# Query copies tied behind the preceding softmax, merge loads tied to other weights, gated sums on GpSimd

## The chip, the cores and the metric

The kernel runs on one core of one Trainium2 chip. The metric is the time of one execution on the device in microseconds; the time before is the median of 3 runs, 2679.12 us (2677.36 to 2681.72).

## The reference

One encoder layer for 2048 tokens of width 1024, all in float32:

```python
h = rms_norm(x, norm_mix)
z = h @ w_in                     # 1024 -> q_a 512, k_a, v_a 128 each, q_b, k_b, v_b 512 each, gates 2 x 1024
y_a = windowed_gqa(q_a, k_a, v_a, sink)      # 8 heads, 2 key heads, |t-s| <= 128, ALiBi, a sink logit
y_b = neighborhood_attn(q_b, k_b, v_b, rpb)  # 8 heads on a 32 x 64 grid, 8 x 16 neighbours, position bias
merged = sigmoid(g_a + b) * (y_a @ w_proj_a) + sigmoid(g_b + b) * (y_b @ w_proj_b)
x = x + merged @ w_out
h2 = rms_norm(x, norm_mlp)
x = x + square(relu(h2 @ w_up)) @ w_down     # 1024 -> 4096 -> 1024
return rms_norm(x, norm_final)
```

## The kernel before

Every float32 product is made of three matmuls of rounded parts (`mm3`, L201: high by high, high by low, low by high). ScalarE rounds a tile to its high part, VectorE (in places GpSimd) subtracts it from the tile for the low part (`split`, L276; the attention's `ph` and `pl`). The four large projections (in, gate, up and down in part, out) use seven block products in place of eight, with sums of blocks made ahead by VectorE; the out-projection's seven are run in the order n = 1, 2, 5, 6, 3, 7, 4.

The stages follow one another on TensorE: in-projection (to 525 us), attention A (32 units of 4 heads by 128 queries), attention B (32 units of a head by a group of columns, with four row groups as its four tiles), merge (gating and out-projection, once per half m of the tokens), up, down. In attention A and B, matmuls of the gates and of the first out-going projection are put in between as fill work (tiles `mm`, `z`).

A scheduler places the instructions. It runs the program on a model of the engines and issues what is ready; the result is a fixed order for each engine, and on the chip each engine takes its instructions strictly in that order. `tc.issue_after(ins)` tells the scheduler to place what follows behind `ins` in the order of the engine that `ins` is on, with no semaphore. Tiles come from rings: a load into a ring's buffer waits until the buffer's last reader is through. Loads are issued by SyncE, in order, and each waits for the one before it on the same of eight semaphores, taken in turn.

An attention unit loads its queries (`load_q`, `q`, a ring of 3 buffers). The tile has two copies, z = 0 as loaded and z = 1 with the upper and the lower 64 partitions swapped and the halves apart; `turn_q` makes z = 1 with one copy on ScalarE (L834) and one on VectorE (L835). For each of four tiles a matmul with z = 0 and one with z = 1 make scores in a bank `s` (a ring of 3 banks); VectorE adds the bias and takes the maximum (L863 in A, L1112 in B), ScalarE negates it (L866, L1115) and takes the exponential with its sum (L870, L1118), VectorE makes the reciprocal (L872, L1120), and GpSimd scales the four tiles (L874, L1123). Then TensorE transposes the tile in pieces (`pt`), ScalarE and VectorE split those (`ph` L900, `pl` L901; in B `phb` L1159, `plb` L1160), and TensorE multiplies them with V (`av`). In B, GpSimd also makes the bias tables (L1078).

In the merge, `gated(f)` makes 128 features for 1024 tokens: loads of the gate `zg` and of the other branch's gated product `zp` (tiles `z`, 4 and 2 buffers), 24 matmuls with a slice of `w_pb`, the gate times the product on VectorE (L1640), and the sum of both into `m` (L272). `out_operands` makes the operands of the out-projection from `m` (`pgl`, weights `wo_d`), `out_products` multiplies, and VectorE adds the result to the rows of x (`xr`, L272). Finished rows are stored (`x2d`), normalised (L230 to L241), and turned by VectorE's transposes in groups g of 256 features into `h2d` (`turned_out`, L253). `beside_out(m)` is stepped once for each n; in m = 1 it steps `up_right`, which prepares up's left weights (`uraw`, `ubh`).

Of the kernel before, what the change touches and what calls it, by code (L numbers as in the profile page):

```python
# [8 lines left out]
F32 = mybir.dt.float32  # L9
# [13 lines left out]
P = 128  # L23
KC = D // P
NB = 4
BT = 512
# [66 lines left out]
def encoder_layer(ctx, tc, x, norm_mix, w_in, b_gate, sink, rpb, w_pa, w_pb, w_out,  # L93
# [733 lines left out]
    def load_q(pl, tag, src):  # L827

        q = T(pl, [P, 2, 4, P], F32R, tag, 3)
        return q, SY.dma_start(q[:, 0].bitcast(F32), src).ins  # L830

    def turn_q(q):

        A.copy(q[0:64, 1], q[64:128, 0].bitcast(F32))  # L834
        V.tensor_copy(out=q[64:128, 1], in_=q[0:64, 0].bitcast(F32))  # L835

    kas = [T(ap_, [P, S], F32R, f"ka{g}", 1) for g in range(2)]
    vas = [T(ap_, [P, 16, P], F32R, f"va{g}", 1) for g in range(2)]
# [5 lines left out]
    def attn_a(u, g, i):  # L844
        c0, c1 = (1 if i == 0 else 0), (2 if i == 15 else 3)
        lo, hi = c0 * P, c1 * P
        n = hi - lo
        if bias_a[g] is None:
            make_bias_a(g)
        base = (i - 1) * P  # L850
        q, ins = load_q(ap_, "qa", qs_a[g][i // 8][:, :, i % 8])
        began.append(ins)
        yield
        turn_q(q)
        ka, v = kas[g], vas[g]
        s = T(ap_, [P, 4, 384], F32, "sa", 4)
        st = T(ap_, [P, 8, 4], F32, "sta", 8)
        mx, nm, sm, es, ri = (st[:, k, :] for k in range(5))
        for h in range(4):
            ps = psum("s", 3)  # L860
            for z in range(2):
                PE.matmul(ps[:, :n], q[:, z, h, :], ka[:, base + lo : base + hi], start=z == 0, stop=z == 1)
            V.tensor_tensor_reduce(out=s[:, h, lo:hi], in0=ps[:, :n], in1=bias_a[g][:, h, lo:hi], scale=1.0,  # L863
                                   scalar=sink_t[:, 4 * g + h : 4 * g + h + 1], op0=ALU.add, op1=ALU.max,
                                   accum_out=mx[:, h : h + 1])
        A.activation(nm, mx, AF.Copy, scale=-1.0)  # L866
        V.tensor_tensor(out=es, in0=sink_t[:, 4 * g : 4 * g + 4], in1=mx, op=ALU.subtract)
        A.activation(es, es, AF.Exp)
        for h in range(4):
            A.activation(s[:, h, lo:hi], s[:, h, lo:hi], AF.Exp, bias=nm[:, h : h + 1], accum_out=sm[:, h : h + 1])  # L870
        V.tensor_tensor(out=sm, in0=sm, in1=es, op=ALU.add)
        V.reciprocal(ri, sm)  # L872
        for h in range(4):
            G.tensor_scalar(s[:, h, lo:hi], s[:, h, lo:hi], ri[:, h : h + 1], 0.5, ALU.mult, ALU.mult)  # L874
        yield
        po = [None]

        def result(c, ph, pl):
            if c == c0:
                po[0] = psum("av", 2)  # L880
            PE.matmul(po[0], v[:, i - 1 + c, :], ph, start=c == c0, stop=False)
            PE.matmul(po[0], v[:, i - 1 + c, :], pl, start=False, stop=c == c1 - 1)
            if c < c1 - 1:
                return
            e = u % 2 * 64
            t = (ya if u % 4 < 2 else yb)[e : e + 64]
            A.copy(t, po[0][64 - e : 128 - e, :])
            V.tensor_tensor(out=t, in0=po[0][e : e + 64, :], in1=t, op=ALU.add)
            flush(queue=SY)
            put(y_a[g].rearrange("(h d) t -> d h t", d=64)[:, :, i * P : (i + 1) * P],  # L890
                t.rearrange("d (h q) -> d h q", h=4))

        for c in range(c0, c1):
            pt = psum("pt", 2)
            for h in range(4):
                last = PE.transpose(pt[:, h * P : (h + 1) * P], s[:, h, c * P : (c + 1) * P], ident).ins
            marks.append(last)
            ph = T(ap_, [P, 512], F32R, "ph", 3)
            pl = T(ap_, [P, 512], F32R, "pl", 3)
            A.copy(ph, pt)  # L900
            V.tensor_tensor(out=pl, in0=pt, in1=ph.bitcast(F32), op=ALU.subtract)  # L901
            behind(lambda c=c, ph=ph, pl=pl: result(c, ph, pl))
# [143 lines left out]
    bp = pools(s_b, "right", ("masks", "braw0", "biass", "stb", "kb0", "qb", "biasl", "braw1", "kb1"), "b")  # L1046
    bp.update(pools(s_b, "left", ("sb0", "sb1", "vb0", "vb1", "sb2", "vb2", "phb", "plb"), "b"))
    boff, bstart, btotal = bias_layout()
    last_exp, n_raw = [None], [0]
    masks = T(bp, [P, btotal], F32, "masks", 1)  # L1050
    with tc.issue_after(began[20]):
        SY.dma_start(masks, mask_b)
# [36 lines left out]
    def attn_b(n_u, h, j, k, bias):  # L1089
# [25 lines left out]
        A.activation(nm, mx, AF.Copy, scale=-0.125)  # L1115
        for i in range(4):
            n = B_NR[i] * w
            last_exp[0] = A.activation(s[i][:, :n], s[i][:, :n], AF.Exp, bias=nm[:, i : i + 1], scale=0.125,  # L1118
                                       accum_out=sm[:, i : i + 1]).ins
        V.reciprocal(ri, sm)  # L1120
        for i in range(4):
            n = B_NR[i] * w
            G.tensor_scalar(s[i][:, :n], s[i][:, :n], ri[:, i : i + 1], 0.5, ALU.mult, ALU.mult)  # L1123
# [228 lines left out]
    def up_right(m):  # L1352
# [3 lines left out]
        def block(b, j, p):  # L1356
            SY.dma_start(b, h2d[2 * m + j][p * BT : (p + 1) * BT, :].rearrange("(k p) t -> p k t", p=P))
            if m:
                for k in range(4):
                    by_gain(b[:, k], 4 * p + k)  # L1360
            return b
# [13 lines left out]
        def gained(t, p):  # L1375
            for k in range(4):
                by_gain(t[:, k], 4 * p + k)
# [34 lines left out]
        yield  # L1412
        with tc.issue_after(last_left[0]):
            gained(t, 0)
            gained(b12, 0)
        b22 = block(up_rings["raw"](), 1, 1)
        gained_less(t, b22, 1, t)
        parts(6, t)
# [95 lines left out]
        yield  # L1514

    ORDER_O = (1, 2, 5, 6, 3, 7, 4)
    wo_dma, last_left = [None], [None]

    def out_operands(ms):

# [61 lines left out]
    def beside_out(m):  # L1582

        loads = load_y(1) if m == 0 else up_start()
        for n in range(7):
            if n == 1:
                with tc.issue_after(wo_dma[0]):
                    rows[1].extend(x_row(m, 1, t) for t in range(4))
            elif m == 0 and n in (3, 5):
                y_behind[0] = wo_dma[0]  # L1590
                state["y"] = next(loads)
            elif m == 1 and n:
                if n < 5:
                    next(loads)
                elif n == 6:
                    free = [T(p4x, [P, 2, 2, BT], F32, f"m{t}", 1).rearrange("p a b c -> p a (b c)") for t in (0, 1)]
                    turned_last(0, lambda g: free[g // 2][:, g % 2])
            yield

    def x_row(m, i, t):  # L1600
        row0 = (2 * m + i) * BT + t * P
        return load_tile(p4x, "xr", 8, xf[row0 : row0 + P])

    def turned_last(i, own):

        for g in range(4):
            turned_out(h2d[2 + i], own(g), rows[i], g)

    state = {"y": next_y}
# [1 line left out]
    for m in range(2):  # L1611
        ys = state["y"]
        ms = [T(p4x, [P, 2, 2, BT], F32, f"m{i}", 1) for i in range(4)]
        hls = {}
        operands = out_operands(ms)
        n_g = [0]
        old, rows = rows, [[], []]

        def gated(f):

            with tc.issue_after(wo_dma[0]) if m and f < 4 else nullcontext():
                gated_at(f)

        def gated_at(f):

            if f % 2 == 0:
                hls[f // 2] = slice_of([(cols(w_pb[0], (f + i) * P), 4) for i in range(2)])
            hl, c0 = hls[f // 2], 4 * (f % 2)
            g, ga = T(wp, [P, 2, BT], F32, "z", 4), T(p4, [P, 2, BT], F32, "z", 2)
            for j in range(2):  # L1630
                SY.dma_start(g[:, j], zg[2 * m + j][1][f * P : (f + 1) * P, :])
            for j in range(2):
                last_dma[0] = SY.dma_start(ga[:, j], zp[2 * m + j][f]).ins
            for j in range(2):
                ps = bank_at(n_g[0] % 4)
                n_g[0] += 1
                for c in range(4):
                    t = ys[j][c // 2]
                    mm3(ps, hl[:, 0, c0 + c, :], hl[:, 1, c0 + c, :], t[:, 0, c % 2], t[:, 1, c % 2], c == 0, c == 3)
                V.scalar_tensor_tensor(out=g[:, j], in0=g[:, j], scalar=1.0, in1=ps, op0=ALU.add, op1=ALU.mult)  # L1640
            add(V, ms[f // 2][:, f % 2], ga, g)

        for f in range(8):
            if m:
                i = f // 4
                turned_out(h2d[i], T(p4x, [P, 2 * BT], F32, "ht", 1), old[i], f % 4)
            gated(f)
            if f == 3:
                with tc.issue_after(last_dma[0]):
                    ready = [next(operands), next(operands)]  # L1650
            if f >= 4:
                with tc.issue_after(last_dma[0]):
                    rows[0].append(x_row(m, 0, f % 4))
        if m == 1:
            s_pg.close()
            s_w.close()

        def all_operands():
            yield from ready
            yield from operands  # L1660

        beside = beside_out(m)
        out_products(m, all_operands(), rows, beside)
# [8 lines left out]
        right = next(rights)  # L1672
    for _ in rest:
        pass
    turned_last(1, lambda t: hu())
    s_hu.close()
    s_wo.close()
    up_homes("bh3", "chunk", "bh7", "bh4")
    for m in range(2):
        if m:  # L1680
            right = next(rights)
# [203 lines left out]
```

## Time and profile before

| | |
|---|---|
| median of 3 runs | 2679.12 us (2677.36 to 2681.72) |
| profiled execution | 2687.74 us |
| its span in the profile | 2686.0 us |
| mean granted TensorE clock | 0.987 |
| busy: TensorE, VectorE, ScalarE, GpSimd | 2574.7, 1743.1, 1351.5, 355.8 us |
| in-projection, attention A, attention B | 0 to 525, 525 to 815, 815 to 1160 us |
| merge, up, down | 1160 to 1440, to 2068, to 2686 us |

The page gives each engine's busy time and the chain of work that ended last. A group's row reads: line, engine, operation, output and inputs with shapes, count, busy time, mean duration in ns, then the engine's idle time just before these instructions and what ended it. A row of the waits reads: engine, tile, line, what ended the wait, the total in us, how often, the longest. A row of the windows gives for each engine the busy time and the count of instructions, then the clock (1.00 is full), the busy share of the DMA engines and their rate. A timeline's row begins with start and duration in us.

### The profile page before, as it was taken

To read this page: it belongs to the slowest core of one execution; us is meant where nothing else is said; L and a number is where in the kernel's file an instruction comes from. 1 tells how busy PE (TensorE), PEld (TensorE's weight loads), DVE (VectorE), ACT (ScalarE), POOL (GpSimd) and SP (SyncE) were. 2 spreads that over 40 slices of the span, in tenths; PEclk is the share of its full clock that TensorE was granted. 3 is DMA by queue.
4 is the path that set the end of the run, shared out by engine and by line. 5 is a ranking of instruction groups with operands and counts; after the bars stand their busy time and mean duration, and the time that the engine had idled before them with its cause. 6 is when DMAs were issued, how large, how long until landed. Compare 5 with 4: busy or idle time off the path is not lost.

```text
span 2686.0 us, 34629 instructions
## 1 busy us (share of the span) xinstructions
PE 2574.7 (96%) x11936; PEld 2128.8 (79%) x11936; DVE 1743.1 (65%) x2781; ACT 1351.5 (50%) x2409; POOL 355.8 (13%) x482
## 2 busy tenths in 40 slices
PE   7999999989999989999999999999999999999998
PEld 5788888867777777788777788888887888888887
DVE  8856677566665666656577766786666535545766
ACT  6365555467766665532426555554445233322444
POOL 1001001133345645300000000000000000000001
PEclk9999999999999999999999999999999999999999
DMA  5767778753335676567996765764436935445555
GB/s 181 222 203 254 254 249 271 233 156 93 83 109 170 183 234 198 179 223 262 321 331 210 262 215 205 260 232 145 165 110 231 325 137 172 143 149 171 179 193 169
DMA packets 345776, 542.73 MB, mean 202 GB/s; under 512 B 31688, under 2 KB 151992, under 8 KB 344448
## 3 DMA queue, kind: packets, MB, share of 16 engines
q1 hardware_dynamic: 328416, 499.99, 57.4%
q10 hardware_dynamic: 10944, 24.12, 2.5%
q0 software_dynamic: 6240, 16.40, 1.9%
q8 instruction: 94, 1.54, 0.2%
q14 instruction: 82, 0.67, 0.1%
HBM read 353.69 MB, written 186.71 MB: 201 GB/s over the span
## 4 chain that ended last, share of the span: by engine, by line
PE 73%; DMA 11%; DVE 7%; ACT 4%; issue 3%; SPq 1%; POOL 0%; ACTq 0%; DVEq 0%; POOLq 0%
PE b L283 15%; PE b L282 15%; PE b L281 15%; PE zb L281 4%; PE zb L283 4%; PE zb L282 4%; DMA qb<-qs_b 4%; PE mm L202 2%; DMA qa<-qs_a 2%; PE mm L203 2%; PE mm L204 2%; PE av L1133 1%; PE b L202 1%; PE b L203 1%; PE b L204 1%
## 5 line engine op out<-in xcount | busy, mean ns | idle before, releaser
L282 PE MATMUL b<-dwh,dah 128*128 128x512 f32 x896 | 348.7, 389 | 0.4 <-DVE dwh L278 0.4
L283 PE MATMUL b<-dwh,dah 128*128 128x512 f32 x896 | 347.7, 389 | 0.0
L281 PE MATMUL b<-dwh,dah 128*128 128x512 f32 x896 | 338.4, 389 | 1.7 <-ACT dwh L277 1.7
L277 ACT CAST dah<-da 128x1024 fp32r<-128x1024 f32 (+1 forms) x128 | 121.1, 947 | 367.6 <-PE b L283 245.0
L281 PE MATMUL zb<-zh,zwhl 128*128 128x512 f32 x728 | 284.4, 391 | 4.8 <-DVE zc L272 1.7
L283 PE MATMUL zb<-zh,zwhl 128*128 128x512 f32 x728 | 283.4, 391 | 1.3 <-DVE zwhl L278 1.2
L282 PE MATMUL zb<-zh,zwhl 128*128 128x512 f32 x728 | 284.6, 391 | 0.0
L278 DVE TENSOR_TENSOR dah<-da,dah 128x1024 fp32r<-128x1024 f32 (+1 forms) x128 | 139.3, 1090 | 217.3 <-ACT dah L277 214.3
L281 PE MATMUL b<-ubh,uwhlb 128*128 128x512 f32 x592 | 231.7, 392 | 5.2 <-DVE uc L272 2.4
L282 PE MATMUL b<-ubh,uwhlb 128*128 128x512 f32 x592 | 231.9, 392 | 3.4 <-DVE ubh L278 3.4
L283 PE MATMUL b<-ubh,uwhlb 128*128 128x512 f32 x592 | 230.2, 391 | 0.0
L281 PEld LDWEIGHTS b<-dwh,dah 128*128 128x128 f32 x896 | 168.1, 188 | 36.9 <-ACT dwh L277 2.1
L282 PEld LDWEIGHTS b<-dwh,dah 128*128 128x128 f32 x896 | 168.2, 188 | 35.8 <-DVE dwh L278 0.8
L283 PEld LDWEIGHTS b<-dwh,dah 128*128 128x128 f32 x896 | 168.2, 188 | 34.9
L272 DVE TENSOR_TENSOR uc<-b,uc 128x512 f32<-128x512 f32 x160 | 109.2, 690 | 117.2 <-PE b L283 110.8
L202 PE MATMUL mm<-zh,whl 128*128 128x512 f32 x368 | 159.5, 434 | 10.9 <-DVE z L1007 6.4
L281 PEld LDWEIGHTS zb<-zh,zwhl 128*128 128x128 f32 x728 | 136.7, 188 | 35.6 <-ACT zc L488 2.5
L283 PEld LDWEIGHTS zb<-zh,zwhl 128*128 128x128 f32 x728 | 136.7, 188 | 30.3 <-DVE zwhl L278 2.6
L282 PEld LDWEIGHTS zb<-zh,zwhl 128*128 128x128 f32 x728 | 136.7, 188 | 27.8
L203 PE MATMUL mm<-zh,whl 128*128 128x512 f32 x368 | 147.5, 401 | 0.0
L204 PE MATMUL mm<-zh,whl 128*128 128x512 f32 x368 | 147.3, 400 | 0.0
L281 PEld LDWEIGHTS b<-ubh,uwhlb 128*128 128x128 f32 x592 | 111.9, 189 | 29.7 <-issue 2.8
(264 smaller groups left out, 5759.9 us busy)
## 6 DMA issues: line engine op xcount, KB each, us to landing
at<-uc SPq DMA_DIRECT2D x224, 256.0 KB, 2.1
da<-at SPq DMA_DIRECT2D x96, 512.0 KB, 3.5
dw<-in_w_down_dram SPq DMA_DIRECT2D x160, 256.0 KB, 4.5
uraw<-in_w_up_dram SPq DMA_DIRECT2D x32, 1024.0 KB, 6.4
pgl<-wo_d SPq DMA_DIRECT2D x28, 1024.0 KB, 7.5
zraw<-in_w_in_dram SPq DMA_DIRECT2D x24, 1024.0 KB
z<-zg SPq DMA_DIRECT2D x64, 256.0 KB, 4.0
qs_a<-ze SPq DMA_DIRECT2D x32, 256.0 KB, 5.5
```

Source lines behind the costliest of these rows:

```text
L202: PE.matmul(ps, lh, rh, start=first, stop=False)
L203: PE.matmul(ps, lh, rl, start=False, stop=False)
L204: PE.matmul(ps, ll, rh, start=False, stop=last)
L272: return eng.tensor_tensor(out=out, in0=a, in1=b, op=op).ins
L277: rounded[0] = A.copy(hi, src).ins
L278: return eng.tensor_tensor(out=lo, in0=src, in1=hi.bitcast(F32), op=ALU.subtract).ins
L281: PE.matmul(ps, lh, rh, start=first, stop=False, skip_group_check=True)
L282: PE.matmul(ps, lh, rl, start=False, stop=False, skip_group_check=True)
L283: PE.matmul(ps, ll, rh, start=False, stop=last, skip_group_check=True)
L1133: PE.matmul(po[0][:, i0 * P : (i0 + ni) * P], v[:kp, c, :], src[:kp, o : o + ni * P], start=first[0], stop=(c == 7 and z == 1), skip_group ...
```

## The change

Five edits. The copies of `turn_q` are placed behind the last exponential (ScalarE) and the reciprocal (VectorE) of the unit whose softmax was written before them, in A and B alike. The preparation of up's weights (`up_right`) gives way once more, and `beside_out` steps it at n = 5 and 6 of the second half. Of the first four groups of turned rows at the end of the second half, three are made there, in `m1` and `ht` in place of `m0` and `m1`, and the fourth later in the ring `hu`; two of up's rings are opened in another order. The gated sum moves from VectorE to GpSimd. The first four gating loads of the second half are tied behind the weights of n = 3, in place of the last weights; their weight slices (`slice_of`) are tied to nothing.

```diff
+    softmax = [None, None]
     def turn_q(q):
-        A.copy(q[0:64, 1], q[64:128, 0].bitcast(F32))
-        V.tensor_copy(out=q[64:128, 1], in_=q[0:64, 0].bitcast(F32))
+        with tc.issue_after(softmax[0]) if softmax[0] else nullcontext():
+            A.copy(q[0:64, 1], q[64:128, 0].bitcast(F32))
+        with tc.issue_after(softmax[1]) if softmax[1] else nullcontext():
+            V.tensor_copy(out=q[64:128, 1], in_=q[0:64, 0].bitcast(F32))
...
         for h in range(4):
-            A.activation(s[:, h, lo:hi], s[:, h, lo:hi], AF.Exp, bias=nm[:, h : h + 1], accum_out=sm[:, h : h + 1])
+            softmax[0] = A.activation(s[:, h, lo:hi], s[:, h, lo:hi], AF.Exp, bias=nm[:, h : h + 1],
+                                      accum_out=sm[:, h : h + 1]).ins
         V.tensor_tensor(out=sm, in0=sm, in1=es, op=ALU.add)
-        V.reciprocal(ri, sm)
+        softmax[1] = V.reciprocal(ri, sm).ins
...
-            last_exp[0] = A.activation(s[i][:, :n], s[i][:, :n], AF.Exp, bias=nm[:, i : i + 1], scale=0.125,
-                                       accum_out=sm[:, i : i + 1]).ins
-        V.reciprocal(ri, sm)
+            softmax[0] = A.activation(s[i][:, :n], s[i][:, :n], AF.Exp, bias=nm[:, i : i + 1], scale=0.125,
+                                      accum_out=sm[:, i : i + 1]).ins
+        softmax[1] = V.reciprocal(ri, sm).ins
...
         with tc.issue_after(last_left[0]):
             gained(t, 0)
+        yield
+        with tc.issue_after(last_left[0]):
             gained(b12, 0)
+        yield
         b22 = block(up_rings["raw"](), 1, 1)
...
             elif m == 0 and n in (3, 5):
                 y_behind[0] = wo_dma[0]
+                if n == 3:
+                    z_behind[0] = wo_dma[0]
                 state["y"] = next(loads)
             elif m == 1 and n:
                 if n < 5:
                     next(loads)
-                elif n == 6:
-                    free = [T(p4x, [P, 2, 2, BT], F32, f"m{t}", 1).rearrange("p a b c -> p a (b c)") for t in (0, 1)]
-                    turned_last(0, lambda g: free[g // 2][:, g % 2])
+                else:
+                    next(started[0])
+                if n == 6:
+                    free = T(p4x, [P, 2, 2, BT], F32, "m1", 1).rearrange("p a b c -> p a (b c)")
+                    turned_last(0, lambda g: free[:, g] if g < 2 else T(p4x, [P, 2 * BT], F32, "ht", 1), (0, 1, 2))
...
         def gated(f):
-            with tc.issue_after(wo_dma[0]) if m and f < 4 else nullcontext():
-                gated_at(f)
-
-        def gated_at(f):
-
             if f % 2 == 0:
                 hls[f // 2] = slice_of([(cols(w_pb[0], (f + i) * P), 4) for i in range(2)])
+            with tc.issue_after(z_behind[0]) if m and f < 4 else nullcontext():
+                gated_at(f)
+
+        def gated_at(f):
+
...
-            add(V, ms[f // 2][:, f % 2], ga, g)
+            add(G, ms[f // 2][:, f % 2], ga, g)
...
+    turned_last(0, lambda t: hu(), (3,))
     turned_last(1, lambda t: hu())
     s_hu.close()
     s_wo.close()
-    up_homes("bh3", "chunk", "bh7", "bh4")
+    up_homes("bh3", "bh4", "chunk", "bh7")
```

ScalarE's order at the start of attention A, as a difference (`qa` and `qb` are query tiles of A and B, the numbers are those of the tiles; `sta_4560` belongs to unit 0, `ze` and `z` to the in-projection's end and the fill work):

```order
-L834 CAST qa_4555<-qa_4555 64x512
-L834 CAST qa_4590<-qa_4590 64x512
 L422 CAST ze_4426<-zb_4219 128x4x128
 L422 CAST ze_4443<-zb_4234 128x4x128
-L834 CAST qb_7530<-qb_7530 64x512
-L834 CAST qb_7538<-qb_7538 64x512
-L834 CAST qb_7581<-qb_7581 64x512
-L866 ACTIVATE sta_4560<-sta_4560 128x4
+L870 ACTIVATE sta_4560<-sta_4560 128x4
 L465 ACTIVATE z_5499<-mm_5474,bg 128x512
```

Before, five copies, three of them for B's first units, stood ahead of unit 0's negated maximum (now L870); now none of the five does.

VectorE's order in the middle of A, before. `sta_4764`, `sta_4836`, `sta_4908` and `sta_4980` are four units in their order, each with its L863, its reciprocal L872 and its `pl` evictions; `qa_4975` is the query tile of the unit after these four, `sta_5041`:

```order
L872 RECIPROCAL sta_4764<-sta_4764 128x4
L901 TENSOR_TENSOR pl_4747<-pt_4741,ph_4746 128x512
L901 TENSOR_TENSOR pl_4800<-pt_4794,ph_4799 128x512
L863 ISA sa_4835,sta_4836<-s_4849,biasa_517_4754,sink_t 128x256
L863 ISA sta_4836 128x1
L867 TENSOR_TENSOR sta_4836<-sink_t,sta_4836 128x4
L835 CAST qa_4975<-qa_4975 64x512
L888 TENSOR_TENSOR ya_4531<-av_4738,ya_4531 64x512
L871 TENSOR_TENSOR sta_4836<-sta_4836 128x4
```

Now, around the same copy:

```order
L906 TENSOR_TENSOR pl_5091<-pt_5085,ph_5090 128x512
L876 TENSOR_TENSOR sta_4980<-sta_4980 128x4
L877 RECIPROCAL sta_4980<-sta_4980 128x4
L839 CAST qa_4975<-qa_4975 64x512
L906 TENSOR_TENSOR pl_5103<-pt_5097,ph_5102 128x512
L867 ISA sa_5040,sta_5041<-s_5042,biasa_517_4754,sink_t 128x384
L867 ISA sta_5041 128x1
```

The copy stood in the softmax of the unit three ahead of its own; it now stands directly behind the reciprocal of the unit one ahead, and its own unit's maximum (L867) follows. On TensorE the three matmuls with z = 0 for which there are banks stand ahead of the copy's consumers, and those with z = 1 follow behind a few products of other units.

VectorE's order in the second half's out-projection, before (`b_13066` to `b_13090` hold n = 6, `b_13196` to `b_13217` hold n = 5, `pgl` are operands, `uS`, `uraw` and `ubh` are up's left weights):

```order
L278 TENSOR_TENSOR pgl_13256<-m_1494_12620,pgl_13256 128x1024
L278 TENSOR_TENSOR pgl_13260<-m_1495_12621,pgl_13260 128x1024
L272 TENSOR_TENSOR xr_12870<-b_13066,xr_12870 128x512
L272 TENSOR_TENSOR xr_12916<-b_13074,xr_12916 128x512
L272 TENSOR_TENSOR xr_12968<-b_13082,xr_12968 128x512
L272 TENSOR_TENSOR xr_13014<-b_13090,xr_13014 128x512
L272 TENSOR_TENSOR uS_13360<-uraw_13289,uraw_13291 128x1024
L272 TENSOR_TENSOR xr_13104<-b_13196,xr_13104 128x512
L272 TENSOR_TENSOR xr_13106<-b_13203,xr_13106 128x512
```

And now:

```order
L272 TENSOR_TENSOR m_1494_12620<-m_1494_12620,m_1492_12618 128x2x512
L272 TENSOR_TENSOR m_1492_12618<-m_1494_12620,m_1492_12618 128x2x512
L272 TENSOR_TENSOR xr_13104<-b_13196,xr_13104 128x512
L272 TENSOR_TENSOR xr_13106<-b_13203,xr_13106 128x512
L272 TENSOR_TENSOR m_1495_12621<-m_1495_12621,m_1493_12619 128x2x512
L272 TENSOR_TENSOR m_1493_12619<-m_1495_12621,m_1493_12619 128x2x512
L272 TENSOR_TENSOR xr_13108<-b_13210,xr_13108 128x512
L278 TENSOR_TENSOR pgl_13168<-m_1492_12618,pgl_13168 128x1024
```

The evictions of n = 5 stood behind those of n = 6 and a difference of up's weights; they now stand ahead of the operands `pgl_13168`.

More of the change, by code (lines that the diff above doesn't have):

```diff
@@ L1048, in encoder_layer @@
     boff, bstart, btotal = bias_layout()
-    last_exp, n_raw = [None], [0]
+    n_raw = [0]
     masks = T(bp, [P, btotal], F32, "masks", 1)
@@ L1516, in encoder_layer @@
     ORDER_O = (1, 2, 5, 6, 3, 7, 4)
-    wo_dma, last_left = [None], [None]
+    wo_dma, z_behind, last_left = [None], [None], [None]
     def out_operands(ms):
@@ L1602, in x_row, with turned_last @@
         return load_tile(p4x, "xr", 8, xf[row0 : row0 + P])
-    def turned_last(i, own):
-        for g in range(4):
+    def turned_last(i, own, gs=range(4)):
+        for g in gs:
             turned_out(h2d[2 + i], own(g), rows[i], g)
@@ L1619, in gated @@
         def gated(f):
-            with tc.issue_after(wo_dma[0]) if m and f < 4 else nullcontext():
+            if f % 2 == 0:
+                hls[f // 2] = slice_of([(cols(w_pb[0], (f + i) * P), 4) for i in range(2)])
+            with tc.issue_after(z_behind[0]) if m and f < 4 else nullcontext():
                 gated_at(f)
         def gated_at(f):
-            if f % 2 == 0:
-                hls[f // 2] = slice_of([(cols(w_pb[0], (f + i) * P), 4) for i in range(2)])
             hl, c0 = hls[f // 2], 4 * (f % 2)
```

## The prediction

> **What bounds the kernel now.** I read the page first: which engine is full, and what the chain that ends last consists of.
>
> ```profile
> PE 2574.7 (96%) x11936; PEld 2128.8 (79%) x11936; DVE 1743.1 (65%) x2781; ACT 1351.5 (50%) x2409; POOL 355.8 (13%) x482
> PE 73%; DMA 11%; DVE 7%; ACT 4%; issue 3%; SPq 1%; POOL 0%; ACTq 0%; DVEq 0%; POOLq 0%
> ```
>
> TensorE is busy 96% of 2686.0 us: all that can be won without removing matmuls is its 111 us of idle time, and what a lowered clock costs. The change removes no matmul, so the question is where those 111 us lie. The view by windows, cut at the stages (in-projection up to 525, 32 units of attention A, 32 of B, merge, up), says so:
>
> ```profile
> core 0: us, PE busy (x) PEld busy (x) DVE busy (x) ACT busy (x) POOL busy (x), PEclk, DMA share, GB/s
> 525.00:815.00 290.00, 261.76 (x1299) 210.78 (x1299) 187.37 (x512) 196.31 (x504) 104.77 (x152) 0.97 0.41 121
> 815.00:1160.00 345.00, 312.01 (x1803) 269.47 (x1802) 217.66 (x520) 215.54 (x514) 180.15 (x220) 0.97 0.65 194
> 1160.00:1300.00 140.00, 140.00 (x635) 116.32 (x634) 82.43 (x107) 40.82 (x62) 2.23 (x4) 1.00 0.73 262
> 1300.00:1490.00 190.00, 169.96 (x708) 137.53 (x707) 138.37 (x210) 86.59 (x134) 7.56 (x12) 0.94 0.85 288
> ```
>
> TensorE idles 28.2 us in A, 33.0 in B and 20.0 from 1300 to 1490. These are the stages that the change edits. What TensorE waits for there is in the view of waits, first for 525 to 1165, then for 1160 to 1490:
>
> ```profile
> PE s L1107 <- DVE stb L1112: 12.1, 8, 3.6
> PE s L862 <- DVE sta L863: 10.1, 8, 6.5
> PE av L882 <- DVE pl L901: 9.1, 12, 3.2
> PE av L1133 <- DVE plb L1160: 7.7, 13, 2.2
> PE av L881 <- ACT ph L900: 6.8, 7, 1.8
> ...
> PE b L281 <- issue: 5.6, 1, 5.6
> PE b L202 <- DVE xr L272: 4.8, 1, 4.8
> ```
>
> In attention it never waits for a query load; it waits for VectorE and ScalarE, which evict its banks. What these two wait for is in the groups by line, each shape apart (525 to 1165):
>
> ```profile
> L834 ACT CAST qa<-qa 64x512 fp32r<-64x512 f32 x32 | 19.8, 620 | 21.9 <-DMA qa<-qs_a 20.3 <-PE pt L896 1.2
> L834 ACT CAST qb<-qb 64x512 fp32r<-64x512 f32 x32 | 19.8, 619 | 55.6 <-DMA qb<-qs_b 55.5
> L835 DVE CAST qb<-qb 64x512 fp32r<-64x512 f32 x32 | 20.8, 651 | 54.9 <-DMA qb<-qs_b 54.7
> L835 DVE CAST qa<-qa 64x512 fp32r<-64x512 f32 x32 | 17.4, 544 | 46.9 <-DMA qa<-qs_a 46.6
> ```
>
> The swapping copies stand in the engines' order two or three units ahead of their use, where their load has hardly been issued. The engine stops there, and the evictions behind it wait although their banks are full. That is the stall that the change is aimed at.
>
> **Part 1, the copies behind the softmax.** Nothing is added or removed: 64 copies on each engine stay, each now directly behind the exponentials (ScalarE) or the reciprocal (VectorE) of the unit ahead. By then their load is a unit old.
>
> At the start three copies for B stand ahead of unit 0's softmax:
>
> ```profile
> 546.00:556.00 10.00, 5.17 (x12) 3.97 (x13) 4.34 (x15) 5.32 (x15) 3.80 (x8) 0.52 0.86 271
> ```
>
> TensorE does 5.17 us of work in these 10, and at half clock, so about 2.6 us of it is clock. With the 6.5 us wait that is 9.1; the next thing late is unit 1's own copy and evictions, for which I leave 1. Term: −8.
>
> For the rest, A and B hold 28.2 + 33.0 − 6.5 = 54.7 us of idle TensorE. How much hangs on the copies? VectorE is idle 635 − 187.4 − 217.7 = 230 us there and 46.6 + 54.7 = 101.3 of it are before these copies (44%); ScalarE is idle 223 us and 20.3 + 55.5 = 75.8 of it are (34%). I take their mean, 40%, as the share of TensorE's waits for these engines that goes: −21.9. It is a choice: a stopped engine need not stop TensorE, and a stop that goes uncovers the next wait.
>
> Idle time costs clock as well:
>
> ```profile
> 853.60:857.00 3.40, 1.29 (x9) 1.06 (x8) 1.37 (x5) 1.20 (x4) 0.05 (x1) 1.00 0.53 148
> 857.00:860.40 3.40, 3.40 (x16) 3.29 (x15) 2.86 (x11) 2.96 (x10) 3.40 (x5) 0.50 0.71 290
> ```
>
> A stretch of 3.4 us in which TensorE worked 1.29 is followed by 3.4 us at half clock. The mean of 0.97 over 635 us is 19 us lost at most; 0.48 × 10 = 4.8 of them lie in the start's window, so about 14 are left, of which again 40% go: −5.6. [...]
>
> What part 1 adds is a wait: unit u+1's second-half score matmuls can't start before unit u's softmax is done. The units become a serial chain, and its length is the risk.
>
> ```profile
> L863 DVE CUSTOM_DVE_ANT_0 sa<-s,biasa,sink_t 128x384 f32<-128x384 f32 x112 | 64.9, 612 | 12.9 <-PE s L862 11.0 <-PE pt L896 1.5
> L870 ACT ACTIVATE sa<-sa,sta 128x384 f32<-128x384 f32 x112 | 67.8, 608 | 1.1
> L870 ACT ACTIVATION_READ_ACCUMULATOR sa<-sa,sta 128x1 f32 x128 | 24.2, 189 | 0.0
> L862 PE MATMUL s<-ka,qa 128*128 128x384 f32 x224 | 56.3, 352 | 9.8 <-DVE sta L863 9.6
> ...
> 700.30 0.18 DVE L872 RECIPROCAL sta<-sta 128x4 f32<-128x4 f32 x1
> 700.57 0.69 DVE L901 TENSOR_TENSOR pl<-pt,ph 128x512 fp32r<-128x512 f32 x1
> 700.67 1.72 POOL L874 TENSOR_SCALAR sa<-sa,sta 128x384 f32<-128x384 f32 x3 [3.64 <-ACT ph L900]
> ```
>
> Per unit: last score 0.35, four bias-and-maximum steps 2.45, the negation about 0.2, four exponentials with their sums 4 × 0.80 = 3.2, ScalarE's copy 0.62: 6.8 us. A handoff between engines is 0.19 (the reciprocal's end at 700.48 to GpSimd at 700.67); four make 7.6. TensorE has 261.8 / 32 = 8.2 us of work per unit in A and 312.0 / 32 = 9.75 in B (whose steps are alike; I take the same chain). So the chain costs nothing in the forecast: other units' transposes, products with V and the fill work cover it, with 0.6 us to spare in A and 2.1 in B. Without that cover each microsecond over is 32 us per branch. One lo-part eviction (0.69) that stands ahead already takes A's reserve.
>
> The copy's new place speaks against it in another way. GpSimd's four normalising scalings start on that same reciprocal, and next to GpSimd the copy can be stopped:
>
> ```profile
> 928.91 4.00 DVE L835 CAST qb<-qb 64x512 fp32r<-64x512 f32 x1 [0.71 <-DMA qb<-qs_b]
> 929.61 3.00 POOL L1078 TENSOR_TENSOR biass<-braw,masks 128x288 f32<-128x288 f32 x3
> L835 DVE CAST qb<-qb x32: 420/422/3998, 547.6 to 1117.9; 64x512 fp32r<-64x512 f32 x32
> ```
>
> 0.42 us is its median, 4.00 its worst, under three bias additions. The mean of 651 ns above is 7.4 us over 32 × 0.42 in all. Bounds: 0 if the copy starts first (VectorE's next instruction began at 700.57, GpSimd at 700.67), 2.3 us a unit if it waits out four scalings of about 0.57. I take 0: it is nearest to the first row, and the chain's ScalarE copy (0.62) covers 0.2 of it. [...]
>
> **Part 2, gated sums on GpSimd.**
>
> ```profile
> L272 DVE TENSOR_TENSOR m<-z,z 128x1024 f32<-128x1024 f32 x16 | 19.5, 1220 | 2.2 <-DMA z<-zp 1.9
> L179 POOL TENSOR_TENSOR whl<-raw,whl 128x1024 fp32r<-128x1024 f32 x14 | 33.8, 2416 | 32.9 <-ACT whl L178 23.9 <-DVE sta L867 8.9
> ```
>
> Sixteen sums of 1.22 us leave VectorE and take about 2.4 each on GpSimd, which has 2.2 us of work in 1160 to 1300. A gating step of TensorE is 24 matmuls of 140.00 / 635 = 0.22 us, 5.3 us, so GpSimd keeps up. The loads into the two buffers that a sum frees are issued 1.2 us later, with SyncE's further loads behind them; they have a step of 5.3 us for it. The last sum's columns are first used in n=2's second half, three halves of 24 matmuls (16 us) on. Cost 0, bounds 0 to +5; gain 0, as TensorE did not wait in 1160 to 1300.
>
> **Part 3, merge loads, groups of turned rows, up's weights.** The loads of the second gating are tied to n=3's weights instead of the last ones, so twelve of them pass the last four weight loads on SyncE's queue; the slices pass even more. Two stalls hang on these:
>
> ```profile
> 1310.40 0.63 ACT L230 ACTIVATE junk<-xr 128x512 bf16<-128x512 f32 x1 [9.48 <-DMA z<-zg]
> 1402.17 2.49 DVE L272 TENSOR_TENSOR xr<-b,xr 128x512 f32<-128x512 f32 x4
> 1404.57 1.23 DVE L272 TENSOR_TENSOR uS<-uraw,uraw 128x1024 f32<-128x1024 f32 x1
> 1310.00:1320.00 10.00, 7.21 (x21) 5.80 (x22) 5.01 (x11) 7.69 (x18) 2.20 (x4) 0.66 0.92 319
> 1400.00:1410.00 10.00, 4.42 (x13) 3.22 (x12) 10.00 (x13) 1.33 (x2) 0.00 (x0) 0.66 1.05 402
> ```
>
> At 1310 ScalarE stands 9.48 us behind a late gate load, then TensorE waits 4.8 for an eviction. At 1401 TensorE waits 5.6 (the view says "issue") while VectorE evicts n=6 and makes a weight difference before n=5's rows; in the new order n=5's evictions come first. Clock: 7.21 × 0.34 + 4.42 × 0.34 = 4.0. Pool: 4.8 + 5.6 + 4.0 = 14.4. VectorE is full at 1400, so something else is late next: I take 70%, −10, bounds −14 to +5 (the last weights then stand behind the twelve loads). The transition to up (1460 to 1490) keeps its other waits; the eight scalings of up's weights and the row transposes move by a few us in the same order: 0.
>
> **The sum.** −8 − 21.9 − 5.6 − 10 = −45.5. The profiled execution took 2687.74 us (span 2686.0 and 1.74 around it), so 2642 by profile. It is 8.6 above the median of the runs, 2679.12; on that scale 2634.
>
> **The rivals.** *TensorE becomes the bound.* All named waits go: 9 + 54.7 + 14 + 14.4 = 92, time 2587. For it: chain 7.6 below 8.2. Against: ScalarE and VectorE also wait for each other without copies. Chance 0.12. *Hidden anyway.* Stopped engines had slack; the stop turns into waiting for the softmax. Only the start and half of the merge go: −13, 2666. For it: more than half of VectorE's idle time is not before a copy. Chance 0.18. *The chain sets the pace.* Three lo-part evictions (2.1) stand in each unit's softmax on VectorE, and in B a collision of about 1 us with GpSimd, by the 928.91 row. A: 7.6 + 2.1 = 9.7 against (290 − 8) / 32 = 8.8 now, +29; B: 10.7 against 345 / 32 = 10.8, −3; with −8 and +2 for a merge that gives its stalls back as later weights: +20, 2699. It decides from 9.1 us a unit in A, two evictions. Chance 0.18. *The copies are still early* because the tie names only an earlier instruction of the same engine: the orders of both engines speak against it, one copy stands behind each softmax; no chance of its own.
>
> **How the numbers follow.** The forecast has 0.52, with 2612 to 2662 as its own range (share of waits 20% to 70%, merge 0 to −14). About 0.2% (5.4 us) is what a measurement can tell. Faster: 0.51 + 0.12 + 0.13 of the hidden case = 0.76. Same: 0.01 + 0.05 = 0.06. Slower: 0.18. The range of 8 in 10 leaves out most of the first rival and the chain's worse half: 2606 to 2692.
>
> **What would show it.** Right: no idle time before the copies on either engine, TensorE's idle in 525 to 1160 down from 61 to about 32, the half clock at 546 gone, one of the two merge waits gone. Wrong: scores waiting for a copy (`s <- ACT q` or `DVE q`) by more than 30 us in all, copies of 1 to 4 us in most units, a pitch above 9.1 us in A, or the idle time in 1300 to 1490 at 20 us or more.

## The result and the profile after

The changed kernel takes 2665.29 us (2660.37 to 2669.77, 5 runs) against 2679.12 before: 0.9941 of the time, 95% interval 0.9921 to 0.9962, 13.8 us faster where 45 were forecast and 2606 was the range's low end, 2692 its high. Its profiled execution took 2660.37 us, the shortest of its five, while that of before (2687.74) was longer than all of its runs. The two profiles therefore lie 27 us apart. A second profile of the kernel before (below) took 2679.21 us, close to the median; it is 8.5 us shorter, and its attention 9.5 us, and it is the one to compare with. Attention of one and the same kernel can thus differ by 9.5 us between two executions, so smaller differences between single profiles are not safe by themselves.

The windows from the first score matmul of A to the last product with V of B, in the second profile of before and in the changed kernel (columns as above):

```profile
536.50:1161.70 625.20, 572.68 (x3114) 479.92 (x3113) 405.09 (x1031) 411.56 (x1019) 285.73 (x372) 0.97 0.54 160
```

```profile
533.60:1153.80 620.20, 567.29 (x3114) 472.70 (x3113) 398.60 (x1031) 411.32 (x1019) 288.77 (x372) 0.98 0.55 162
```

The same 3114 matmuls; TensorE idles 52.5 us before and 52.9 after. The 5.0 us between the two are in its busy time, that is, in the clock, and they are less than the spread just named. In these two profiles part 1 did not reduce the idle time of attention, though it took the stops away. The copies' rows after, in the groups by line from 525 to 1150:

```profile
L839 DVE CAST qb<-qb 64x512 fp32r<-64x512 f32 x32 | 20.2, 631 | 1.0
L837 ACT CAST qb<-qb 64x512 fp32r<-64x512 f32 x32 | 19.8, 618 | 0.8
L837 ACT CAST qa<-qa 64x512 fp32r<-64x512 f32 x32 | 19.8, 617 | 4.6 <-DMA qa<-qs_a 3.9
L839 DVE CAST qa<-qa 64x512 fp32r<-64x512 f32 x32 | 13.5, 421 | 4.2 <-DMA qa<-qs_a 3.2
```

The idle time just before these copies, 179 us in the first profile of before and 167 in the second, is now 10.6 us. What TensorE waits for now, from the view of waits, first 525 to 1140, then 1140 to 1470:

```profile
PE s L866 <- DVE qa L839: 19.3, 17, 1.9
PE s L1112 <- DVE qb L839: 7.3, 7, 1.9
PE pt L901 <- POOL sa L879: 6.1, 4, 3.9
PE s L1112 <- DMA vb<-vs_b: 4.4, 1, 4.4
...
PE b L281 <- DMA pgl<-wo_d: 8.2, 2, 7.4
PE b L281 <- DVE uc L272: 2.3, 1, 2.3
```

The scores wait for the copies themselves, 17 times in A's 32 units. The stages split, in A (first to last score) of the second profile of before and of the changed kernel:

```profile
536.50:801.50 265.00, 240.32 (x1202) 193.86 (x1201) 177.44 (x493) 187.29 (x484) 103.48 (x148) 0.97 0.39 112
```

```profile
533.60:820.90 287.30, 254.93 (x1260) 202.42 (x1259) 172.36 (x495) 191.44 (x490) 105.67 (x148) 0.97 0.36 106
```

A is 22 us longer: 8.98 us a unit in place of 8.28. TensorE did 14.6 us more in it (58 matmuls of fill and of earlier units that were done in B's time before are now done in A's) and idled 7.7 us more (24.7 to 32.4). The rest of attention, from A's last score to B's last product, is 27 us shorter; in the same two kernels:

```profile
801.50:1161.70 360.20, 332.36 (x1913) 286.06 (x1912) 227.65 (x539) 224.28 (x536) 182.25 (x224) 0.97 0.65 196
```

```profile
820.90:1153.80 332.90, 312.37 (x1855) 270.27 (x1855) 226.23 (x537) 219.88 (x529) 183.10 (x225) 0.98 0.71 210
```

58 matmuls fewer, 7.3 us less idle time. So A's loss and B's gain in idle time cancel.

In the merge, both old waits are gone (4.8 at the second gating, 5.6 behind n=6), and the row with `pgl<-wo_d` stands in the place of the second: 7.4 us for weights, one product earlier, ahead of n=6.

### The profile page after: what moved, and what is told of

Same layout as the page of the kernel before. It is cut to its first block, busy times and chain, and to the rows that moved or that the text cites. A ratio compares the mean times of both kernels' runs of the same rounds, so it can differ in the third digit from the quotient of the medians.

```text
span 2658.6 us, 34718 instructions
## 1 busy us (share of the span) xinstructions
PE 2565.4 (96%) x11936; PEld 2120.1 (80%) x11936; DVE 1724.2 (65%) x2765; ACT 1351.0 (51%) x2409; POOL 399.4 (15%) x498
```

## The experiments

All times are medians on chips shared with the kernel before, which took 2675.5 to 2678.3 there; ratios are to that, with the 95% interval. The experiments ran on three chips, and the changed kernel's own time was taken apart from them, so a difference of two medians can be some 4 us off what the ratios give; where it matters both are named.

**The ties alone** (the kernel before with part 1, nothing else).

> The kernel before with the ties of the query copies alone. Serial chain (attention A is paced by score, softmax, copy; only B gains): A's waits for the copies L839 stay near 19 us in all, B's idle time falls by 13 or so, total 2669 us (-10). Rival, fill work (the ties do nothing for A or B, fill matmuls only moved from B into A): 2678, idle time of A and B together unchanged at 61. Rival, merge alone (all of the gain is made behind 1160 us): 2679.

Measured: 2672.16 us, ratio 0.9982 (0.9973 to 0.9991), 4.7 us faster, half of the 10 forecast. A's waits for the copies are as forecast. The waits from 525 to 1160:

```profile
PE s L866 <- DVE qa L839: 19.7, 17, 1.9
PE s L1112 <- DVE qb L839: 9.2, 8, 1.9
```

The waits for the copies come with the ties, whatever the merge does.

**All but the ties** (`turn_q` as before, the other edits kept).

> The changed kernel with the copies untied, the other edits kept. Serial chain: both engines stop before the copies for about 170 us again, attention ends some 10 us later than in the changed kernel, total 2673. Merge alone: no change against the changed kernel, 2665.

Measured: 2666.18, ratio 0.9960 (0.9947 to 0.9972), 10.7 faster, though forecast at 2673; the rival of that forecast, 2665, was nearer. With the run above, some 5 us of the gain are the ties' and about 10 the other edits'.

**A free, B tied.**

```diff
-    def turn_q(q):
...
+    def turn_q(q, lag):
+
+        for e, ins in zip(ended, softmax):
+            e.append(ins)
+        tied = [e[-lag] if lag and len(e) >= lag else None for e in ended]
...
-        turn_q(q)
+        turn_q(q, 0)
...
-        turn_q(q)
+        turn_q(q, 1)
```

The first call is A's, the second B's; `lag` says how many units ahead the softmax of the tie lies, and 0 leaves the copies untied.

> The changed kernel with A's copies untied, B's tied. Serial chain: TensorE no longer waits 19 us for A's copies, and the waits behind late loads (10 to 15 us) come back, with the start's stall gone since B's copies no longer stand there: 2655. Fill work: 2665, as the changed kernel.

Measured: 2644.86, ratio 0.9880 (0.9867 to 0.9894), 10 us below the forecast. Against the changed kernel, A's tie costs 16 us by the ratios and 20 by the medians (18 by the spans of the two profiles). Against the kernel without ties, on the same chip, B's tie gains 21 us. VectorE stops before A's loads again, and still A is faster (the row by line, A's window, and the rest of attention):

```profile
L842 DVE CAST qa<-qa 64x512 fp32r<-64x512 f32 x32 | 16.2, 507 | 51.4 <-DMA qa<-qs_a 51.1
534.50:797.80 263.30, 241.42 (x1202) 194.73 (x1201) 177.47 (x490) 185.86 (x481) 103.79 (x148) 0.97 0.39 113
797.80:1136.30 338.50, 320.29 (x1913) 278.24 (x1912) 228.79 (x542) 226.12 (x539) 182.64 (x224) 0.99 0.71 209
```

The rest of attention holds the same 1913 matmuls as in the second profile of before, and takes 338.5 us where it took 360.2: 9.6 us less idle time and 12.1 less busy time. So the stops did cost TensorE time in B, and a tie one unit ahead gains there about what it loses in A.

**Two units ahead in A** (`turn_q(q, 2)` in A, 1 in B).

> The changed kernel with A's copies tied behind the softmax of two units ahead in place of one. Serial chain: the copy is done a unit early, its load is 8 us old, neither wait remains: idle time of A from 32 to 15 or less, total 2650. Fill work: 2665. If the load has not landed by then, stops before the copies of over 20 us return and the time is about 2660.

Measured: 2625.87, ratio 0.9810 (0.9797 to 0.9823), far below the forecast of 2650. It is 35 us below the changed kernel by the ratios and 39 by the medians, for a tie that names the softmax one unit earlier. The groups by line, then A and all of attention:

```profile
L840 ACT CAST qa<-qa 64x512 fp32r<-64x512 f32 x32 | 19.8, 620 | 5.7 <-DMA qa<-qs_a 4.9
L842 DVE CAST qa<-qa 64x512 fp32r<-64x512 f32 x32 | 14.9, 466 | 5.8 <-DMA qa<-qs_a 4.9
533.50:780.20 246.70, 234.97 (x1202) 191.79 (x1201) 177.27 (x490) 186.84 (x481) 105.62 (x148) 0.99 0.42 121
533.50:1119.10 585.60, 556.57 (x3114) 471.21 (x3113) 405.69 (x1031) 412.87 (x1019) 288.23 (x372) 0.99 0.59 172
```

Of the two waits, the stops are down to 11.5 us and the scores' waits for A's copies are gone: A's idle time is 11.7 us where it was 24.7 before and 32.4 after, and the clock is 0.99. The engines still stop for two loads each; all others had landed.

**Two units ahead in B as well.**

> A's and B's copies tied behind the softmax of two units ahead. Serial chain: B's waits for its copies (9.0 us in the kernel with two ahead in A alone) go as A's did: 2615 to 2620. Rival, B is not a chain (its TensorE work of 9.75 us a unit covers the softmax): no change against 2626. Rival, late loads: B's loads take 5 us and more to land, both engines stop before them again: 2630 or more.

Measured: 2622.95, ratio 0.9794 (0.9777 to 0.9811), against 0.9797 to 0.9823: not told apart. The scores' 9.0 us of waits for B's copies are gone, as the chain's case said, but not the time. B's scores end 7.3 us earlier, but the last product with V comes within 0.1 us of the other kernel's. The matmuls between first and last score fell from 1735 to 1687; what the scores won was filled by work that stood behind them afterwards.

**ScalarE's copy in A done twice**, in the changed kernel and with two ahead.

```diff
             A.copy(q[0:64, 1], q[64:128, 0].bitcast(F32))
+            if twice:
+                A.copy(q[0:64, 1], q[64:128, 0].bitcast(F32))
```

> The changed kernel with ScalarE's copy of A's queries done twice (same data, same place). Serial chain: that copy or the reciprocal's branch beside it ends the chain; 0.62 more in ScalarE's branch, which ends some 0.2 to 0.3 us ahead of VectorE's, is 0.3 to 0.6 a unit for 32 units: +10 to +20, 2675 to 2685. No chain (engines with slack): +0 to 3, 2665 to 2668.

> The same doubled copy in the kernel with two ahead in A. Serial chain: the copy is off the chain, +0 to 4 (20 us more of a ScalarE that is 70% busy): 2626 to 2630. No chain: the same cost as in the changed kernel.

Measured: 2709.55 and 2635.40, ratios 1.0119 (1.0100 to 1.0137) and 0.9837 (0.9815 to 0.9859): +44 and +9.5 us by the medians (+48 and +7 by the ratios) for the same 32 copies of 0.62. A's windows:

```profile
534.10:870.40 336.30, 276.23 (x1280) 220.35 (x1279) 179.21 (x501) 212.16 (x524) 108.03 (x149) 0.92 0.31 92
```

```profile
534.30:790.40 256.10, 238.89 (x1202) 192.16 (x1201) 178.91 (x490) 204.38 (x512) 105.15 (x148) 0.99 0.40 117
```

A work of 20 us costs 49 us of A where the tie is one unit ahead, 9.4 where it is two. The direction is the chain's. Both sizes were forecast too small, and the second case, forecast at 0 to 4, shows that the copy was not free there either. In the first the extra 0.9 us a unit is not the copy: the order also moved, TensorE's wait for GpSimd's scalings (`pt`) rose from 6.1 to 36.5 us in A, its waits for the copies all but went, and the clock fell to 0.92. So this pair agrees with a chain that paces A, but does not show it by itself, nor by how much; the run with two ahead is the stronger evidence.

**The merge's edits one at a time**, each undone in the kernel with two ahead in A.

> The kernel with two ahead in A, the gated sums back on VectorE. If the stall at the second gating went because VectorE was freed: it comes back, +7 (2633). If it went because the gating loads come earlier: no change, 2626.

Measured: 2620.60, ratio 0.9788 (0.9773 to 0.9802), 5.3 us faster by the medians, which neither case foresaw; the intervals of the two kernels just touch. The stall at the second gating stays away with the sums on VectorE, and the wait for weights falls from 7.2 to 2.8 us:

```profile
PE b L281 <- DMA pgl<-wo_d: 2.8, 1, 2.8
```

> The kernel with two ahead in A, the second half's first gating loads and slices tied behind the last weights as before, all else as changed. If the late gate load made the stall at the second gating: it comes back, +7, and the wait for the weights at the second out-projection (7 us) goes: 2626 in all, one exchanged for the other. If the freed VectorE took the first stall away: 2619.

Measured: 2630.46, ratio 0.9823 (0.9807 to 0.9840), 4.6 us slower by the medians. The waits from 1120 to 1490 are the two old ones, and the weights' is gone:

```profile
PE b L281 <- issue: 5.0, 1, 5.0
PE b L202 <- DVE xr L272: 4.4, 1, 4.4
```

So the ties of the loads, not the sums, removed both stalls and brought the third. By landmarks in the traces the second gating is 7.0 us longer with the old tie and the second out-projection 2.3 shorter.

**The kernel before, once more.**

> The kernel before, unchanged, for a second profile. The profiled execution of 2687.74 us lies 8 to 11 above the median of its runs; if one stage varies, its landmarks show which: attention (loads) by the theory that stops before late loads are chance, merge or up by the other.

Measured: 2679.21, a single execution. Against the first profile it is 4.6 us shorter in A and 4.9 in the rest of attention, and within 0.4 in every stage behind. The long execution was longer in attention only.

**Both together.**

> Both branches two units ahead and the gated sums on VectorE: the gains of the two single edits (-3 and -5 against two ahead in A) add up if they are independent: 2618. If the sums' gain was the arrival of the last weights by chance: 2623.

Measured: 2613.24, ratio 0.9757 (0.9739 to 0.9775): 65 us faster than before, 49 (by the ratios) to 52 faster than the changed kernel, and the best of all. The gain of the sums looks larger than additive (9.7 here, 5.3 above), but the 4 us between the two are within the noise. By the traces' landmarks 7.3 of it lie in the second out-projection, where the wait for weights is down to 1.1 us, and the rest is in attention and ahead of it, which this edit does not touch.

**The same, with the second gating's loads tied behind n=5's weights** in place of n=3's.

> The same with the second half's gating loads tied behind n=5's weights in place of n=3's. If the loads' lead is what takes the stall at the second gating away and their crowding of the queue what makes the wait for the last weights: between the two ties both go, 2613. If the lead is then too short: the stall of 7 us is back, 2625.

Measured: 2619.03, ratio 0.9779 (0.9761 to 0.9796). It is slower than the run above, and neither case came true: the stall at the second gating did not return with the shorter lead, and the wait for weights did not go but rose to 3.6 us. What exactly delays these weights on SyncE's queue is open: buffers that the sums free later, ahead of them on that queue, and DMA engines that are busy there (share 0.80 in 1332 to 1418 of the changed kernel) both fit, and no run separates them.

## Why the prediction was wrong

**The step that failed** is "the chain costs nothing in the forecast". The chain was put at 7.6 us against 8.2 of work a unit in A, and other work was to cover it. The runs show a chain of about 9 us that is not covered there: A takes 8.98 us a unit, TensorE idles 7.7 us more in it, and the tie one unit earlier takes 34.6 us off attention. That the units are in series can be counted in the traces: in the changed kernel no unit of A begins its first maximum before the reciprocal of the unit ahead is done, and it follows 1.7 us later on the mean; in the second profile of before, and with two ahead, 18 of 31 begin before it. Here is one unit of the changed kernel, VectorE's timeline, ScalarE's, GpSimd's, then TensorE's (`...` stands for rows left out):

```profile
640.83 0.61 DVE L867 CUSTOM_DVE_ANT_0 sa<-s,biasa,sink_t 128x384 f32<-128x384 f32 x1
641.90 0.62 DVE L867 CUSTOM_DVE_ANT_0 sa<-s,biasa,sink_t 128x384 f32<-128x384 f32 x1
642.56 0.69 DVE L893 TENSOR_TENSOR ya<-av,ya 64x512 f32<-64x512 f32 x1
643.28 1.29 DVE L906 TENSOR_TENSOR pl<-pt,ph 128x512 fp32r<-128x512 f32 x2
644.49 0.61 DVE L867 CUSTOM_DVE_ANT_0 sa<-s,biasa,sink_t 128x384 f32<-128x384 f32 x1
648.75 0.18 DVE L877 RECIPROCAL sta<-sta 128x4 f32<-128x4 f32 x1
648.96 0.42 DVE L839 CAST qa<-qa 64x512 fp32r<-64x512 f32 x1
...
645.14 0.20 ACT L870 ACTIVATE sta<-sta 128x4 f32<-128x4 f32 x1 [1.63 <-DVE sta L867]
645.44 0.59 ACT L905 CAST ph<-pt 128x512 fp32r<-128x512 f32 x1
646.03 0.60 ACT L874 ACTIVATE sa<-sa,sta 128x384 f32<-128x384 f32 x1
648.55 0.62 ACT L837 CAST qa<-qa 64x512 fp32r<-64x512 f32 x1
...
649.11 1.29 POOL L879 TENSOR_SCALAR sa<-sa,sta 128x384 f32<-128x384 f32 x2 [5.54 <-DVE sta L877]
...
643.57 0.87 PE L866 MATMUL s<-ka,qa 128*128 128x384 f32 x4
```

From the first maximum at 640.83 to the copy's end at 649.38 are 8.55 us; this is one of the longer units, the median of A is 7.4. Three maxima end by 642.5, and the fourth starts at 644.49: its bank was free when the first maximum was through, but its matmuls, in the row at 643.57, stand behind other work on TensorE, and one `ya` and two `pl` evictions stand ahead of it on VectorE, 2 us in all. On ScalarE a `ph` of 0.6 stands between the negation and the exponentials. Over all units of A, counted in the trace, the mean from the start of the first maximum to the end of the last is 3.4 us where the sum had 2.45; the exponentials take 2.4 where it had 3.2, because each one's read of its sum (0.19, added in the forecast) overlaps with the next one (in the unit above a read runs from 646.54 to 646.73, and the next exponential starts at 646.63); 0.9 lie between maxima and exponentials, 0.7 from there to the reciprocal's end, and 1.7 from there to the next unit's first maximum, together 3.3 where the sum had 1.9. That makes 9.1 us. So most steps are as long as forecast or shorter, and what the sum left out stands between them: other units' instructions on the same engines. The work that was to cover the chain lengthens it. That is the mechanism of the rival "the chain sets the pace", and it acted in A: 8.98 us a unit, between the 8.2 of the forecast and the rival's 9.7. In B, with 9.75 us of work a unit, the units stand in series as well, but a tie one unit ahead costs nothing that a run can tell: it gains 21 us there (A free against no ties), and a second unit of lead changes the time by less than the noise.

One reservation: each of these edits makes the scheduler place all engines' instructions anew, so the 35 us between one and two units ahead are the tie's with all that the order does with it.

**The signs it named.** Of the signs of being right, the idle time before the copies went and one of the two merge waits went; TensorE's idle time in 525 to 1160 fell from 61 to 53 us, not to 32; and the low clock of the start is as in the second profile of before: 0.89 from 536 to 566 in both. Of the signs of being wrong none was reached: scores waited 26.6 us for copies (30 named), A's copies took 0.42 us each, the pitch was 8.98 (9.1 named), and 1300 to 1490 has 13 us of idle time (20 named). The bounds were set too wide to catch a loss of 16 to 20 us in A.

**Part 1's pool and share.** The share of 40% was meant for what goes when the copies no longer stop the engines. With two ahead, attention ends at 585.6 us against 625.2: −39.6, where −8 − 21.9 − 5.6 = −35.5 were forecast. Idle time gave 23.5 of it and clock 16, where about 27 and 8 were forecast (with the start's term split as it was made). So the pool was about right for a tie that costs nothing; that the sum comes so near is in part luck, as the two errors partly cancel. The tie as written took 34.6 of it back (620.2 against 585.6).

**The start.** Term −8, of which at most half came: the first score starts 2.9 us earlier (533.6 against 536.5). The wait of 5.8 us for the first maxima (6.5 in the first profile) is gone, but the first transposes now wait 3.9 us for GpSimd's scaling; TensorE works 24.7 of the 30 us from 536 against 23.9 in the second profile of before, at a clock of 0.89 in both. The next thing late was unit 0's own scaling, which I did not look for.

**The clock.** The term of −5.6 was an estimate of mine: the same 40% of the lost clock as of the waits. The clock of attention went from 0.97 to 0.99 with two ahead, where TensorE's idle time fell by 23.5 us (52.5 to 29.0). In the first profile's view of the waits (525 to 1165) none but the start's 6.5 was longer than 3.6 us. The last section has more rows.

**The copy beside GpSimd.** Taken at 0, and right in A: all 32 took 0.42, and the one at 648.96 began 0.15 us ahead of the scalings at 649.11. GpSimd paid a little: the mean of its 128x384 scalings in A is 623 ns, where it was 596 in the first profile of before. In B the copies' mean is 631 ns (651 in the first profile of before). The longest took 3.22 us, from 937.21 to 940.43: GpSimd had begun the first of three bias additions at 937.15, ahead of it, and the last ended at 940.15. In the forecast's row of 4.00 us, GpSimd had begun an addition (`whl`) at 927.26, ahead of the copy, and three bias additions followed it without a gap, the last until 932.61; the copy ended at 932.91. So each of these two copies ended 0.3 us behind the last of three bias additions.

**Gated sums.** Taken at 0 with +5 as the bound; measured +5.3 and +9.7 in the kernels with two ahead, most of it by the wait for weights. The bound was named, the mechanism (what stands behind those loads on SyncE) was waved through with "a step of 5.3 us for it".

**The merge** was forecast at −10; the kernel without ties shows −10.7. The stall at the second gating went (7.5 us by the landmarks), the other was exchanged for the wait for weights, and the transition to up, taken at 0, was about 4 us shorter. So the sum is right in part by luck.

**The rival "hidden anyway"** named 2666 and the time is 2665. The number agrees, the reason only in A, where the stop did turn into waiting for the softmax. In B the stops were not hidden (the tie gains 21 us there), the start gave less than its 8 us, and the merge gave its whole term and not the half.

## What to carry to other kernels

A tie that holds work back until it is needed can make a chain of steps that overlapped before. In A, with 8.2 us of work a unit, a tie one unit ahead did so (0.9941) and one whole unit of lead more removed both the stall and the chain's wait (0.9810); in B, with 9.75, one unit was enough. Reckon such a chain from its first instruction to its last with what stands between its steps on each engine, not from the steps' durations alone, and try the tie in each stage by itself. And take a second profile of the kernel before where the first lies above its own runs' range.

## What the runs showed of the hardware

A longer execution of the same program put its extra 9.5 us in attention alone, the part full of short waits, while all stages behind agreed within 0.4 us. And attention A, where TensorE was kept waiting more by the doubled copy (336 us in place of 287, with another order), lost clock on top, from 0.97 to 0.92, although its matmuls were the same but for 20.

In three windows above the clock was lower where TensorE idled more: it idled 52.5 us of the 625.2 of attention in the second profile of before (8.4%), at a clock of 0.97; 29.0 of 585.6 with two ahead in A (5.0%), at 0.99; and 60.1 of 336.3 in A with the doubled copy (17.9%), at 0.92. In the first profile of before the length of a wait did not tell by itself. From 686.4 to 778.4 TensorE idled 8.9 us, 3.2 of them in one wait, and the clock was 1.00:

```profile
686.40:778.40 92.00, 83.07 (x426) 66.33 (x425) 61.33 (x167) 67.11 (x173) 37.82 (x52) 1.00 0.38 105
```

From 850 to 862 its only wait was 2.1 us, and the clock from 857.0 to 860.4 was 0.50. What decides whether the clock falls was not shown.
